# SwiGLU input products by seven block products instead of eight, on a kernel of two decoder layers

## The chip, the cores and the metric

The kernel runs on one core of a Trainium2 chip, as one program. The metric is device time in microseconds (us), the median of repeated runs. A core has five engines with a queue of instructions each, which run in order and wait for one another through semaphores: TensorE (PE in the profile; PEld is its weight load), VectorE (DVE), ScalarE (ACT), GpSimd (POOL) and SyncE (SP), which here issues the transfers (DMA).

## The reference, cut to what matters

Two layers, each of four stages with a LayerNorm behind each: SwiGLU, a mixer of three attention kinds, cross attention, SwiGLU. 512 tokens, 1024 model columns, 2816 hidden columns, all in float32.

```python
D_MODEL, SEQ, DEPTH = 1024, 512, 2
D_FF = ((8 * D_MODEL // 3 + 255) // 256) * 256          # 2816

def swiglu(x, w_in, w_out):
    a, b = jnp.split(x @ w_in, 2, axis=-1)
    return (jax.nn.silu(a) * b) @ w_out

for l in range(DEPTH):
    x = layer_norm(ALPHA * x + 0.5 * swiglu(x, ffn1_w_in[l], ffn1_w_out[l]), ln_g[l, 0], ln_b[l, 0])
    x = layer_norm(ALPHA * x + hybrid_mixer(x, ...), ln_g[l, 1], ln_b[l, 1])
    x = layer_norm(ALPHA * x + cross_attention(x, mem, ...), ln_g[l, 2], ln_b[l, 2])
    x = layer_norm(ALPHA * x + 0.5 * swiglu(x, ffn2_w_in[l], ffn2_w_out[l]), ln_g[l, 3], ln_b[l, 3])
```

## The kernel before, in words

*Products.* A float32 operand is split into two tiles of type fp32r: H, the rounded value (ScalarE's cast), and L, the rest (VectorE's subtraction). A product is then three matmuls, H with H, H with L and L with H (`mm3`). The weight of a matmul is a 128 x 128 block, its moving operand up to 512 columns wide.

*FFN stage (`Ffn`).* The activations stand transposed, `xTH` and `xTL`: 128 partitions x 8 row tiles x 512 tokens. The 5632 columns of `w_in` are taken in column tiles of 128, 22 of the gate part and 22 of the linear part. Per column tile `w_cols` fetches a raw tile (1 MB holds two column tiles; three buffers, `RAW`), `prep` makes `wH` and `wL` (four buffers each), and `proj_T` runs 8 x 3 matmuls of 512 columns into one PSUM bank (`ps`). `act` then applies silu to the gate bank, multiplies by the linear bank into a scratch tile `scr`, and splits the result into `hH` and `hL`.

*Output product (`out_proj`).* Hidden tiles are the weights now, `w_out` rows move, 512 columns at a time, in two column halves c. In the second half the last four groups are run token tile by token tile, so that the LayerNorm of token tiles 0 and 1 (`ln_half`, `ln_norm`) and their transposes (`transpose_x`) run under the remaining matmuls.

*Stage borders (`enter`).* The next stage's `early` runs its first four column tiles on tokens 0 to 255 while tokens 256 to 511 are still in LayerNorm; their transposes are put between. In `early` the subtraction that makes `wL` is shared, half on VectorE and half on GpSimd (`share`). At the very start `load_x` fetches x in halves, and `prefetch` the first weight tile in halves between them, with ScalarE's and VectorE's work on it pinned to its place in the order.

*What sets the order.* The framework's scheduler orders each engine's instructions by its own model of their times; a wait of one instruction holds all that stand behind it on that engine. Beside the first FFN runs a thread (`consts`, stepped in `tick`) that builds the mixer's bias table: eight heads, each a small matmul (`hot`, `rb`), a copy into the one buffer `F`, and two transfers (`biasD`, `biasT`).

Of the kernel before, what the change touches and what calls it, by code (L numbers as in the profile page):

```python
# [525 lines left out]
class Ffn:  # L526


    def __init__(self, net, l, w_in, w_out, lni):
# [2 lines left out]
        self.start = False

    def cols(self, f, part, share=False):
        if f < 2 and self.start:
            return self.net.w_cols((self.tag, part), self.w_in, part * DFF + f * P, n=P, share=share, pin=f == 0)
        return self.net.w_cols((self.tag, part), self.w_in, part * DFF + f * P, f % 2, share=share)

    def prefetch(self, h):

        n, nc = self.net, self.net.nc
        self.start = True
        if h == 0:
            self.raw0 = n.wp.tile([P, KT, P], F32, tag="raw", name=n.nm("raw"), bufs=RAW)
            self.W0 = [n.wp.tile([P, KT, P], F32R, tag=f"w{i}", name=n.nm(f"w{i}"), bufs=4) for i in "HL"]
        ks = slice(4 * h, 4 * h + 4)
        raw, (H, L) = self.raw0[:, ks], self.W0
        nc.sync.dma_start(raw, self.w_in[h * 512:(h + 1) * 512, 0:P].rearrange("(k p) n -> p k n", p=P))
# [3 lines left out]
    def early(self):  # L552
        n = self.net
        self.first = []
        for f in range(2):
# [720 lines left out]
```

## Time and profile before

| | |
|---|---|
| median of 3 runs | 2267.9 us (2267.69 to 2268.06) |
| the profiled execution, its own time | 2267.45 us |
| its span, first to last instruction | 2265.7 us |
| granted TensorE clock, mean | 0.998 |
| input products of one FFN, 782 to 1010 us | TensorE busy 228.00, VectorE 80.26, ScalarE 67.84 us |
| output product of that FFN, 1010 to 1130 us | TensorE busy 120.00, VectorE 39.17, ScalarE 22.11 us |

Busy times of an engine count its instructions from start to end; matmuls overlap in the pipeline, so TensorE's rate is read from the distance of starts. The four FFN stages lie at the start, at about 774 to 1138, 1138 to 1502 and 1896 to the end. Nearly all instructions of VectorE, ScalarE and GpSimd have one line, L121, a wrapper's, and all matmuls L194: groups are told apart by the tiles' names.

### The profile page before, as it was taken

The numbers are of one execution on the slowest core, as the hardware profiler recorded it, in microseconds if no ns is written. First come the engines' busy times: TensorE is split into PE (matmuls) and PEld (weight loads), VectorE is DVE, ScalarE is ACT, GpSimd is POOL, SyncE is SP. The second block draws the span as 40 slices with busy tenths as digits, with TensorE's granted clock in tenths as the row PEclk, the third lists the DMA queues.
The fourth block names the chain that finished last, engine by engine and source line by source line (L and its number), as shares of the span: only waits on it lengthen the run. The fifth ranks groups of instructions, "written<-read, shape, count | busy, mean of one in ns | idle before, by whom it ended". The sixth has DMA issues, their size and how long they took to land.

```text
span 2265.7 us, 27710 instructions
## 1 busy us (share of the span) xinstructions
PE 2243.9 (99%) x11360; PEld 1896.5 (84%) x11360; DVE 1082.0 (48%) x1696; ACT 756.5 (33%) x1217; POOL 178.9 (8%) x254
## 2 busy tenths in 40 slices
PE   9999999999999999999999999999999999999998
PEld 8788888888788888888888888888887888888887
DVE  3333335677565633332453333367776656333334
ACT  3222212457524232221132222124674333322211
POOL 1000001251010100000010000013300101000000
PEclk9999999999999999999999999999999999999999
DMA  7655333232432365653266553332233314656431
GB/s 252 220 189 195 130 102 103 68 93 82 124 99 69 112 223 187 199 167 107 84 206 200 188 195 112 102 95 80 88 113 94 112 57 155 199 188 201 150 103 47
DMA packets 273251, 310.97 MB, mean 137 GB/s; under 512 B 6330, under 2 KB 231898, under 8 KB 273124
## 3 DMA queue, kind: packets, MB, share of 16 engines
q1 hardware_dynamic: 273124, 309.20, 42.3%
q8 instruction: 89, 1.46, 0.3%
q14 instruction: 38, 0.31, 0.0%
HBM read 305.51 MB, written 3.67 MB: 136 GB/s over the span
## 4 chain that ended last, share of the span: by engine, by line
PE 90%; DVE 6%; issue 1%; POOL 1%; ACT 1%; DMA 0%; DVEq 0%; SPq 0%; ACTq 0%; POOLq 0%
PE ps L194 88%; PE ps L199 2%; DVE wL L121 1%; DVE x_nat L121 1%; DVE st L121 1%; DVE xTL L121 1%; POOL mlrs L121 1%; DVE Cb L121 0%; DMA x_nat<-in_x_dram 0%; ACT e L121 0%; DVE stL L121 0%; DVE mlst L121 0%; DVE hid L121 0%; ACT xTH L121 0%; DVE memT L121 0%
## 5 line engine op out<-in xcount | busy, mean ns | idle before, releaser
L121 DVE TENSOR_TENSOR wL<-raw,wH 128x1024 fp32r<-128x1024 f32 (+2 forms) x387 | 462.2, 1195 | 722.5 <-ACT wH L121 708.5
L121 ACT CAST wH<-raw 128x1024 fp32r<-128x1024 f32 (+2 forms) x387 | 403.3, 1046 | 1167.1 <-PE ps L194 833.0
L194 PE MATMUL ps<-xTH,wH 128*128 128x512 f32 (+1 forms) x2000 | 728.9, 365 | 1.0 <-ACT sc L121 1.0
L194 PE MATMUL ps<-xTL,wH 128*128 128x512 f32 (+1 forms) x2000 | 726.2, 363 | 2.7 <-DVE xTL L121 2.7
L194 PE MATMUL ps<-xTH,wL 128*128 128x512 f32 (+1 forms) x2000 | 725.4, 363 | 0.0
L194 PEld LDWEIGHTS ps<-xTL,wH 128*128 128x128 f32 x2000 | 378.3, 189 | 61.1 <-DVE xTL L121 5.2
L194 PEld LDWEIGHTS ps<-xTH,wH 128*128 128x128 f32 x2000 | 378.1, 189 | 59.2 <-ACT sc L121 1.2
L194 PEld LDWEIGHTS ps<-xTH,wL 128*128 128x128 f32 x2000 | 378.2, 189 | 58.7
L194 PE MATMUL ps<-wH,hH 128*128 128x512 f32 x704 | 274.8, 390 | 0.0
L194 PE MATMUL ps<-wH,hL 128*128 128x512 f32 x704 | 274.3, 390 | 0.0
L194 PE MATMUL ps<-wL,hH 128*128 128x512 f32 x704 | 274.2, 390 | 0.0
L121 DVE TENSOR_TENSOR scr<-scr,ps 128x512 f32<-128x512 f32 x88 | 60.5, 687 | 274.8 <-PE ps L194 272.7
L121 POOL TENSOR_TENSOR rs<-ve,mhalf 128x1 f32<-128x1 f32 x32 | 29.7, 927 | 1771.5 <-DVE ve L121 1771.5
L194 PEld LDWEIGHTS ps<-wH,hL 128*128 128x128 f32 x704 | 132.2, 188 | 27.5
L194 PEld LDWEIGHTS ps<-wL,hH 128*128 128x128 f32 x704 | 132.2, 188 | 27.3
L194 PEld LDWEIGHTS ps<-wH,hH 128*128 128x128 f32 x704 | 132.2, 188 | 27.0
L121 ACT CAST xTH<-ps 128x512 fp32r<-128x512 f32 x64 | 34.8, 589 | 153.5 <-PE ps L199 152.9
L194 PE MATMUL ps<-wH,oT 128*128 128x512 f32 x256 | 81.8, 392 | 0.0
L121 DVE SCALAR_TENSOR_TENSOR x_nat<-ps,x_nat 128x512 f32<-128x512 f32 x64 | 43.6, 686 | 44.9 <-PE ps L194 44.4
L121 DVE TENSOR_TENSOR hL<-scr,hH 128x512 fp32r<-128x512 f32 x88 | 60.2, 684 | 0.0
L194 PEld LDWEIGHTS ps<-wH,oT 128*128 128x128 f32 x256 | 48.1, 188 | 9.7
L121 ACT CAST hH<-scr 128x512 fp32r<-128x512 f32 x88 | 54.6, 620 | 0.0
(222 smaller groups left out, 2229.7 us busy)
## 6 DMA issues: line engine op xcount, KB each, us to landing
raw<-in_ffn_w_in_dram SPq DMA_DIRECT2D x172, 1024.0 KB, 5.1
raw<-in_ffn_w_out_dram SPq DMA_DIRECT2D x40, 1024.0 KB, 5.0
raw<-in_xattn_w_kv_dram SPq DMA_DIRECT2D x16, 1024.0 KB, 5.4
raw<-in_mix_w_in_dram SPq DMA_DIRECT2D x18, 512.0 KB, 5.7
raw<-in_mix_w_in_dram SPq DMA_DIRECT2D x8, 1024.0 KB, 5.2
raw<-in_mix_w_out_dram SPq DMA_DIRECT2D x16, 512.0 KB, 4.7
raw<-in_xattn_w_q_dram SPq DMA_DIRECT2D x8, 1024.0 KB, 5.1
raw<-in_xattn_w_o_dram SPq DMA_DIRECT2D x8, 1024.0 KB, 5.0
```

The costliest lines, as they stand in the source:

```text
L121: return f(*a, **k)
L194: self.nc.tensor.matmul(out, l, r, start=start, stop=stop, **k)
L199: self.nc.tensor.transpose(out, i, ident)
```

## The change

The input product of an FFN is cut in two along its columns (gate part a, linear part b), its rows (1: rows 0 to 511, 2: 512 to 1023) and its tokens (1: 0 to 255, 2: 256 to 511). Of 2 x 2 x 2 = 8 block products, Strassen's scheme (in Winograd's form) makes 7, with sums of blocks as operands. It is done for a group q of 256 gate and 256 linear columns, eleven groups (`Q`). The blocks of w are a1, a2, b1, b2; with s = b1 + b2 the products, each of 2 x 4 x 3 matmuls of 256 columns, are, in the order of the loop in `body`:

| name here | weight side | token side | goes to |
|---|---|---|---|
| X1 | a1 | B11 | gate, tokens 1 (kept as `p1`) |
| W | s = b1 + b2 | T1 | bank W |
| Y2 | s - a1 | T2 | bank Y, then + `p1`, copied to `u2` |
| R | b2 of the group before | T4 | its bank Y: linear, tokens 1 |
| X2 | a2 | B21 | gate, tokens 1, then silu (`gate1`) |
| L | a2 - (s - a1) of the group before | B22 | its bank W: with `u2` the gate, tokens 2 |
| Y3 | a1 - b1 | T3 | bank Y, copied to `u3`, + W: linear, tokens 2 |

So VectorE gets four additions or subtractions of 128 x 1024 per group (s; b1 = a1 - b1; s - a1; a2 - s) and sums of banks (`u2`, `u3`, Y + `p1`), and per FFN the token side's combinations T1 to T4, which `second` makes from token tiles 2 and 3 when they have been transposed. Groups 0 to 3 have X1 and X2 done in `early` (eight products of tokens 1 in place of four column tiles). The hidden values stay in float32, tile `h` per group, and are split into `hH` and `hL` in the output product's first column half. The weight tiles come in two transfers each; the pinning in `prefetch` is gone; `enter` is called when the stage's pools are closed; and the mixer's constant `chunk1` is filled in each mixer rather than once.

```diff
-        if nxt is not None:
-            self.enter(nxt)
     def enter(self, nxt):
+        if nxt is None:
+            return
         last = self.last
         for i, _ in enumerate(nxt.early()):
             self.hold = last
             if i < 2:
-                self.transpose_x(2 + i)
+                nxt.second(2 + i)
...
-        self.chunk1 = c.tile([MLH, S], F32, name="chunk1")
-        nc.gpsimd.memset(self.chunk1, 1.0)
-        nc.gpsimd.memset(self.chunk1.rearrange("h (c n) -> h c n", c=NT)[:, :, 0:1], 0.0)
...
+    EARLY = 4
+    HT = 256
+    Q = FT // 2
...
+    def open(self):
+        n = self.net
+        self.ctx, self.inner = ExitStack(), ExitStack()
+        self.fp = self.ctx.enter_context(n.tc.tile_pool(name=n.nm("ffn"), bufs=1))
+        self.h = {}
+        self.ip = self.inner.enter_context(n.tc.tile_pool(name=n.nm("ffnin"), bufs=1))
+        self.p1 = [self.ip.tile([P, S], F32, name=n.nm("p1")) for _ in range(self.EARLY)]
+        self.sw = self.ip.tile([P, 4, 256], F32, name=n.nm("sw"))
+        self.T = [[self.ip.tile([P, 4, self.HT], F32R, name=n.nm("T")) for _ in range(2)] for _ in range(3)]
...
+    def load(self, q, half):
+        r = self.raw()
+        for part in range(2):
+            self.net.nc.sync.dma_start(r[:, part], self.block(q, part, half))
+        return r[:, 0], r[:, 1]
...
+    def right(self, x):
+        xs = self.net.xTH, self.net.xTL
+        lo, hi, t1, t2 = slice(0, 4), slice(4, 8), slice(0, self.HT), slice(self.HT, S)
+        if x in ("T2", "T3", "T4"):
+            return self.T[int(x[1]) - 2]
+        k, t = {"B11": (lo, t1), "B21": (hi, t1), "B22": (hi, t2), "T1": (lo, t2)}[x]
+        return [m[:, k, t] for m in xs]
+    def product(self, bank, raw, x, start, share=False):
+        n = self.net
+        H, L = n.prep(raw, [4, 256], share)
+        xH, xL = self.right(x)
+        for j in range(2):
+            js = slice(j * P, (j + 1) * P)
+            o = bank[:, j * self.HT:(j + 1) * self.HT]
+            for k in range(4):
+                n.mm3(o, H[:, k, js], L[:, k, js], xH[:, k], xL[:, k], start and j + k == 0, k == 3, skip_group_check=True)
+            n.tick()
...
+    def two(self, name, dt=F32):
+        return self.fp.tile([P, 2, S], dt, tag="h", name=self.net.nm(name), bufs=self.Q + 1)
+    def hid(self, q, t):
+        if q not in self.h:
+            self.h[q] = self.two("h")
+        return self.h[q][:, :, t * self.HT:(t + 1) * self.HT]
...
-        n.tc.keep_in_program_order(nc.scalar.copy(H[:, ks], raw))
-        n.tc.keep_in_program_order(nc.vector.tensor_sub(L[:, ks], raw, H[:, ks].bitcast(F32)))
...
+        self.open()
+        for q in range(self.EARLY):
+            a = self.first if q == 0 else None
+            if a is None:
+                a = self.raw()
+                for h in range(2):
+                    nc.sync.dma_start(a[:, h], self.block(q, 0, h))
+            b = n.bank()
+            self.product(b, a[:, 0], "B11", True, True)
+            nc.scalar.copy(self.p1[q], b)
+            self.product(b, a[:, 1], "B21", False, True)
+            self.gate1(q, b)
+            yield
...
+    def second(self, t):
+        n, nc = self.net, self.net.nc
+        V = nc.vector
+        bs = [n.bank() for _ in range(2)]
+        for h in range(2):
+            for k in range(4):
+                kk = 4 * h + k
+                n.tp(bs[h][:, k * P:(k + 1) * P], n.x_nat[:, t, kk * P:(kk + 1) * P])
+        b1, b2 = [b.rearrange("p (k n) -> p k n", k=4) for b in bs]
+        ts, t1 = slice(t * P, (t + 1) * P), slice((t - 2) * P, (t - 1) * P)
+        tmp = [w[:, i].rearrange("p (k n) -> p k n", k=4) for w in (self.two("tmp"), self.two("tmp")) for i in range(2)]
+        r1, T2, T3, T4 = tmp
+        (H11, L11), (H21, L21) = self.right("B11"), self.right("B21")
+        n.split(n.xTH[:, 4:8, ts], n.xTL[:, 4:8, ts], b2)
+        nc.scalar.copy(r1, b1)
+        V.tensor_sub(T3, b2, r1)
+        V.tensor_sub(r1, r1, H11[:, :, t1].bitcast(F32))
+        V.tensor_sub(r1, r1, L11[:, :, t1].bitcast(F32))
+        n.split(n.xTH[:, 0:4, ts], n.xTL[:, 0:4, ts], r1)
+        V.tensor_sub(T2, b2, r1)
+        n.split(*[m[:, :, t1] for m in self.T[0]], T2)
+        V.tensor_sub(T4, H21[:, :, t1].bitcast(F32), T2)
+        V.tensor_add(T4, T4, L21[:, :, t1].bitcast(F32))
+        n.split(*[m[:, :, t1] for m in self.T[1]], T3)
+        n.split(*[m[:, :, t1] for m in self.T[2]], T4)
...
-        with n.tc.tile_pool(name=n.nm("ffn"), bufs=1) as fp:
-            hH = fp.tile([P, FT, S], F32R, name=n.nm("hH"))
-            hL = fp.tile([P, FT, S], F32R, name=n.nm("hL"))
-            def act(f, pa, pb):
-                s = n.scr()
-                nc.scalar.activation(s, pa, AF.Silu)
-                nc.vector.tensor_mul(s, s, pb)
-                n.split(hH[:, f], hL[:, f], s)
-            for f in range(FT):
-                bs = []
-                for part in range(2):
-                    if f < 2:
-                        W, b = self.first[2 * f + part]
-                        n.proj_T(b, W, 256, 512)
-                    else:
-                        W, b = self.cols(f, part), n.bank()
-                        n.proj_T(b, W, 0, S)
-                    bs.append(b)
-                act(f, *bs)
...
+        V, ACT = nc.vector, nc.scalar
+        prev = None
+        def rest(r):
+            q, Y, b2 = r["q"], r["Y"], r["b2"]
+            self.product(Y, b2, "T4", False)
+            V.tensor_mul(self.hid(q, 0), self.hid(q, 0), self.pair(Y))
+        def last(r):
+            q, W, u2, u3 = r["q"], r["W"], r["u2"], r["u3"]
+            self.product(W, r["s4"], "B22", False)
+            V.tensor_add(u2, W, u2)
+            ACT.activation(self.hid(q, 1), self.pair(u2), AF.Silu)
+            V.tensor_mul(self.hid(q, 1), self.hid(q, 1), self.pair(u3))
+        for q in range(self.Q):
+            a1, b1 = self.load(q, 0)
+            a2, b2 = self.load(q, 1)
+            s = self.sw
+            V.tensor_add(s, b1, b2)
+            p1 = self.p1[q % self.EARLY]
+            if q >= self.EARLY:
+                X = n.bank()
+                self.product(X, a1, "B11", True)
+                ACT.copy(p1, X)
+            W, Y = n.bank(), n.bank()
+            self.product(W, s, "T1", True)
+            V.tensor_sub(b1, a1, b1)
+            V.tensor_sub(s, s, a1)
+            self.product(Y, s, "T2", True)
+            V.tensor_add(Y, Y, p1)
+            u2 = n.scr()
+            ACT.copy(u2, Y)
+            if prev:
+                rest(prev)
+            if q >= self.EARLY:
+                self.product(X, a2, "B21", False)
+                self.gate1(q, X)
+            V.tensor_sub(a2, a2, s)
+            if prev:
+                last(prev)
+            self.product(Y, b1, "T3", False)
+            u3 = n.scr()
+            ACT.copy(u3, Y)
+            V.tensor_add(u3, W, u3)
+            prev = dict(q=q, Y=Y, W=W, b2=b2, s4=a2, u2=u2, u3=u3)
+        rest(prev)
+        last(prev)
+        self.inner.close()
+        with n.tc.tile_pool(name=n.nm("ffnh"), bufs=1) as hp:
+            hs = {}
+            def wsrc(k0, k, c):
+                if c == 0:
+                    q = k0 // 2
+                    hs[q] = hp.tile([P, 2, S], F32R, name=n.nm("hH")), self.two("hL", F32R)
+                    n.split(*hs[q], self.h[q])
+                return n.w_rows(self.tag, self.w_out, k0, k, c * 512, FT)
+            n.out_proj(FT, lambda f, t: [m[:, f % 2, t * P:(t + 1) * P] for m in hs[f // 2]], wsrc, 0.5 / ALPHA,
+                       self.l, self.lni, nxt)
+        self.ctx.close()
+        n.enter(nxt)
...
+        chunk1 = row("chunk1")
+        G.memset(chunk1, 1.0)
+        G.memset(chunks(chunk1)[:, :, 0:1], 0.0)
         nb = row("nb")
-        V.tensor_tensor_scan(nb, n.chunk1, e, 0.0, ALU.mult, ALU.add)
+        V.tensor_tensor_scan(nb, chunk1, e, 0.0, ALU.mult, ALU.add)
```

What the scheduler makes of it. VectorE in the middle of an FFN, before: `wL` for each column tile, and between them, for a gate and a linear tile together, `scr`, silu times the linear bank, and its split.

```order
L121 TENSOR_TENSOR wL_7010<-raw_7007,wH_7009 128x1024
L121 TENSOR_TENSOR scr_6935<-scr_6935,ps_6910 128x512
L121 TENSOR_TENSOR wL_7041<-raw_7038,wH_7040 128x1024
L121 TENSOR_TENSOR hL_6565<-scr_6935,hH_6564 128x512
L121 TENSOR_TENSOR wL_7077<-raw_7074,wH_7076 128x1024
```

Now, in the second FFN from the end of group 0 to group 2: `scr_7785` is u2 of group 0 (it waits for product L of group 0), `h_7462` that group's gate times u3, `sw_7392` is s, `raw_7981` b1 of group 2, `scr_7978` u3 of group 1, `wL_7991` is for product W of group 2, `wL_8021` for its Y2.

```order
L121 TENSOR_TENSOR scr_7785<-ps_7724,scr_7785 128x512
L121 TENSOR_TENSOR h_7462<-h_7462,scr_7816 128x2x256
L121 TENSOR_TENSOR sw_7392<-raw_7981,raw_7984 128x1024
L121 TENSOR_TENSOR raw_7981<-raw_7981 128x1024
L121 TENSOR_TENSOR scr_7978<-ps_7826,scr_7978 128x512
L121 TENSOR_TENSOR wL_7991<-sw_7392,wH_7990 128x1024
L121 TENSOR_TENSOR sw_7392<-sw_7392,raw_7981 128x1024
L121 TENSOR_TENSOR raw_7984<-raw_7984,sw_7392 128x1024
L121 TENSOR_TENSOR wL_8021<-sw_7392,wH_8020 128x1024
```

Three weight splits with two operations between them have become a run of nine in which the weight split that TensorE needs next stands sixth. On TensorE, L of group 0, Y3 of group 1 and W of group 2 follow each other.

ScalarE at the start of the kernel, before: the casts of the first weight tile (`wH_95`, in halves) stand around those of the transposed x.

```order
L121 CAST wH_95<-raw_94 128x512
L121 CAST xTH_91<-ps_100 128x4x128
L121 CAST xTH_91<-ps_107 128x4x128
L121 CAST wH_95<-raw_94 128x512
L121 CAST xTH_91<-ps_118 128x4x128
```

Now:

```order
L121 CAST wH_144<-raw_94 128x1024
L121 CAST wH_174<-raw_94 128x1024
L121 CAST wH_209<-raw_205 128x1024
L121 CAST xTH_91<-ps_96 128x4x128
L121 CAST xTH_91<-ps_103 128x4x128
```

Three weight casts, of which the third reads the second raw tile (group 1), have moved ahead of the first cast of x.

VectorE where the first FFN leaves `early`, now (before, the second token half's `xTL` stood there with nothing but weight halves around it): `raw_460` and `raw_463` are the raw tiles of group 0, `tmp` and `T` belong to `second`.

```order
L121 TENSOR_TENSOR wL_401<-raw_366,wH_400 128x512
L121 TENSOR_TENSOR sw_136<-raw_460,raw_463 128x1024
L121 TENSOR_TENSOR raw_460<-raw_460 128x1024
L121 TENSOR_TENSOR wL_470<-sw_136,wH_469 128x1024
L121 TENSOR_TENSOR sw_136<-sw_136,raw_460 128x1024
L121 TENSOR_TENSOR xTL_92<-ps_337,xTH_91 128x4x128
L121 TENSOR_TENSOR tmp_347<-ps_337,tmp_346 128x512
L121 TENSOR_TENSOR raw_463<-raw_463,sw_136 128x1024
```

The sums of group 0's weights, which wait for its transfers, stand ahead of the whole of `second` there.

More of the change, by code (lines that the diff above doesn't have):

```diff
@@ L435, in load_x @@
             if i >= 2:
-                self.transpose_x(i)
+                nxt.second(i)
             if i in (1, 2):
@@ L531, in __init__ @@
         self.tag = f"ffn{l}{lni}"
[L532 to L537, printed above, removed]
-    def prefetch(self, h):
-        n, nc = self.net, self.net.nc
[L542 to L548, printed above, removed]
-        n.tc.keep_in_program_order(nc.scalar.copy(H[:, ks], raw))
-        n.tc.keep_in_program_order(nc.vector.tensor_sub(L[:, ks], raw, H[:, ks].bitcast(F32)))
@@ L552, in early @@
[L552 to L555, printed above, removed]
-            for part in range(2):
-                W = getattr(self, "W0", None) if f + part == 0 else None
-                W, b = W or self.cols(f, part, True), n.bank()
-                n.proj_T(b, W, 0, 256)
-                self.first.append((W, b))
-                yield
+        self.first = None
+    def open(self):
[7 more added lines that the diff above has]
+        self.T = [[self.ip.tile([P, 4, self.HT], F32R, name=n.nm("T")) for _ in range(2)] for _ in range(3)]
@@ new lines, in block, with raw @@
+    def block(self, q, part, half):
+        c0 = part * DFF + 256 * q
+        return self.w_in[half * 512:half * 512 + 512, c0:c0 + 256].rearrange("(k p) n -> p k n", p=P)
+    def raw(self):
+        n = self.net
+        return n.wp.tile([P, 2, 4, 256], F32, tag="raw", name=n.nm("raw"), bufs=RAW)
+    def load(self, q, half):
[3 more added lines that the diff above has]
+        return r[:, 0], r[:, 1]
@@ new lines, in prefetch @@
+    def prefetch(self, h):
+        if h == 0:
+            self.first = self.raw()
+        self.net.nc.sync.dma_start(self.first[:, h], self.block(0, 0, h))
+    def right(self, x):
[5 more added lines that the diff above has]
+        return [m[:, k, t] for m in xs]
@@ new lines, in hid, with pair, gate1, early @@
+    def hid(self, q, t):
+        if q not in self.h:
+            self.h[q] = self.two("h")
+        return self.h[q][:, :, t * self.HT:(t + 1) * self.HT]
+    @staticmethod
+    def pair(b):
+        return b.rearrange("p (f n) -> p f n", f=2)
+    def gate1(self, q, bank):
+        self.net.nc.scalar.activation(self.hid(q, 0), self.pair(bank), AF.Silu)
+    def early(self):
+        n, nc = self.net, self.net.nc
+        self.open()
[11 more added lines that the diff above has]
+            yield
@@ L595, in __init__, with second @@
         self.w_in, self.w_out = net.A["mix_w_in"][l], net.A["mix_w_out"][l]
+    def second(self, t):
+        self.net.transpose_x(t)
     def early(self):
@@ L707, in body @@
             n.mx_ctx.close()
+        n.enter(nxt)
     def stack(self, b, scale, parts):
@@ L1145, in memory, with second @@
                 n.split(*n.mv[m][c], bs[m])
+    def second(self, t):
+        self.net.transpose_x(t)
     def early(self):
@@ L1186, in body @@
         del n.mk
+        n.enter(nxt)
     def head(self, h):
```

4 lines of the change are left out of this document (1 added, 3 removed).

## The prediction

> **What bounds the kernel now.** I read the page's busy times and chain of waits first, then the timeline inside one FFN's input products, then the groups with shapes kept apart, and last the start and one stage border.
>
> ```profile
> span 2265.7 us, 27710 instructions
> PE 2243.9 (99%) x11360; PEld 1896.5 (84%) x11360; DVE 1082.0 (48%) x1696; ACT 756.5 (33%) x1217; POOL 178.9 (8%) x254
> PE 90%; DVE 6%; issue 1%; POOL 1%; ACT 1%; DMA 0%; DVEq 0%; SPq 0%; ACTq 0%; POOLq 0%
> ```
>
> TensorE is 90% of the chain: work that leaves it shortens the kernel for as long as nobody makes it wait. Inside the input products (timeline; start and duration in us, in brackets the idle time before and who ended it):
>
> ```profile
> 798.82 0.28 PE L194 MATMUL ps<-xTL,wH 128*128 128x256 f32 x1
> 798.94 0.28 PE L194 MATMUL ps<-xTH,wL 128*128 128x256 f32 x1
> 799.06 0.40 PE L194 MATMUL ps<-xTH,wH 128*128 128x512 f32 x1
> 799.33 0.69 DVE L121 TENSOR_TENSOR scr<-scr,ps 128x512 f32<-128x512 f32 x1 [0.72 <-PE ps L194]
> 800.14 0.61 ACT L121 CAST hH<-scr 128x512 fp32r<-128x512 f32 x1
> 800.27 1.23 DVE L121 TENSOR_TENSOR wL<-raw,wH 128x1024 fp32r<-128x1024 f32 x1 [0.25 <-ACT wH L121]
> 801.41 0.68 DVE L121 TENSOR_TENSOR hL<-scr,hH 128x512 fp32r<-128x512 f32 x1
> ...
> 804.54 1.05 ACT L121 CAST wH<-raw 128x1024 fp32r<-128x1024 f32 x1 [3.79 <-PE ps L194]
> 805.50 0.59 ACT L121 ACTIVATE scr<-ps 128x512 f32<-128x512 f32 x1
> 805.63 1.23 DVE L121 TENSOR_TENSOR wL<-raw,wH 128x1024 fp32r<-128x1024 f32 x1 [3.54 <-ACT wH L121]
> 809.98 1.05 ACT L121 CAST wH<-raw 128x1024 fp32r<-128x1024 f32 x1 [3.90 <-issue]
> ```
>
> Prices from here. A 256-column matmul starts every 0.12 us. One column tile, 24 matmuls of 512 columns, takes 809.98 - 804.54 = 5.44 us, 0.2267 each: two halves cost 0.24, 6% more than one whole. A 1024-wide VectorE subtraction takes 1.23, the next independent one starts after 1.14 (800.27 to 801.41), so 0.09 overlaps: 0.60 for 512 independent elements, 0.72 where the next needs the result. The first reader of a finished bank starts 0.27 after the next product does (799.06 to 799.33). ScalarE to VectorE: 0.04. VectorE idles 3.5 us per tile: it hides everything today.
>
> ```profile
> L121 DVE TENSOR_TENSOR wL<-raw,wH 128x1024 fp32r<-128x1024 f32 x346 | 424.6, 1228 | 694.8 <-ACT wH L121 680.8 <-PE ps L199 1.7 <-PE ps L194 1.2
> L121 DVE TENSOR_TENSOR scr<-scr,ps 128x512 f32<-128x512 f32 x88 | 60.5, 687 | 274.8 <-PE ps L194 272.7 <-ACT scr L121 2.1
> L121 DVE TENSOR_TENSOR wL<-raw,wH 128x512 fp32r<-128x512 f32 x33 | 29.8, 904 | 10.1 <-ACT wH L121 10.1
> L121 DVE TENSOR_TENSOR lg<-lg,swden 128x512 f32<-128x512 f32 x24 | 15.0, 685 | 0.1
> L121 POOL TENSOR_TENSOR wL<-raw,wH 128x512 fp32r<-128x512 f32 x31 | 48.5, 1578 | 30.5 <-ACT wH L121 25.8 <-PE ps L194 4.7
> ```
>
> (Groups: count, total and mean ns, idle before.) A plain fp32 operation on two SBUF operands (lg) costs 685 ns, no less than the fp32r one.
>
> **What leaves.** Per FFN before: 40 tiles whole, 4 in halves: 40 x 5.44 + 192 x 0.12 = 240.6 us. After: 11 groups x 7 products x 24 x 0.12 = 221.8. Saved 18.9, four times 75.5 us: an eighth less multiplying, nearly half of it given back to the narrower matmul. The output stage's matmuls stay as they are; there the split of h moves from 22 pieces beside the input products to 11 pieces of 1024 beside the first half of the output product: 2 x 1.14 us of VectorE per 24 x 0.2267 = 5.4 us group, covered; without cover 11 x 1.2. Weight transfers halve (each tile was fetched twice, for TensorE's bound worth nothing).
>
> **What comes in.** VectorE's work per group rises to seven weight splits, four adds of 1024 and five operations of 512: 11 x 1.14 + 5 x 0.60 = 15.5 us at best, against 20.2 us of seven products and 14.4 of the five in groups 0 to 3 (there 9 x 1.14 + 3.0 = 13.3). It fits by sum. The order decides, because each engine runs its queue in order.
>
> *Groups 1 to 3.* Zero is the end of product L (B22). TensorE goes on with Y3 (2.88 us) and reaches W's third matmul, the first that needs wL, at 3.12. VectorE's queue, as the order quoted above has it: u2 0.27-0.96; h, after ScalarE's silu of 0.62, 1.66-2.35; s 2.26-3.49; b1, which overwrites what s reads, 3.52-4.75; u3 4.66-5.35; W's wL 5.26-6.49. TensorE waits 3.44 and ends W at 9.20. Then s-=a1 to 7.75, a2-=s to 9.01, Y2's wL to 10.15; its third matmul (R's first two go ahead) is due at 9.68: 0.54 more. Together 4.0 us, at two places in each FFN: 8 x 4.0 = 32.0. Behind these lines stand R, L and Y3, whose wL come in time.
>
> *Group 3 to 4 and on.* X1 (2.88) stands between Y3 and W: W's wL is due at 6.00, ready at 6.56, Y2's at 9.68 and 10.18: 1.06, four times 4.2. From group 5 on h comes after s, so its silu is not waited for, and a2-=s comes later in the queue: W's wL at 5.61, in time; s-=a1 to 6.88, cast to 7.97, Y2's wL 9.24 against 9.12. I take 0.4 us a group (0 to 1.5, the ends being no wait and one 1024 operation more), 6 x 4 x 0.4 = 9.6; the turn into the output stage 0.3 x 4 = 1.2.
>
> *Entering an FFN from another stage (three).* A border today:
>
> ```profile
> 1134.90 1.44 POOL L121 TENSOR_TENSOR wL<-raw,wH 128x512 fp32r<-128x512 f32 x1
> 1135.11 2.44 DVE L121 SCALAR_TENSOR_TENSOR x_nat<-x_nat,rs,scr 128x512 f32<-128x512 f32 x2
> ...
> 1138.16 0.28 PE L194 MATMUL ps<-xTH,wH 128*128 128x256 f32 x1
> ...
> 1143.80 1.41 DVE L121 SCALAR_TENSOR_TENSOR x_nat<-x_nat,rs,scr 128x512 f32<-128x512 f32 x2
> ```
>
> ```profile
> 777.34 0.87 PE ps L199 x8
> 778.22 2.87 PE ps L194 x24
> ```
>
> (The second fence is the chain: eight transposes 0.87, 24 matmuls 2.87.) LayerNorm ends 7.0 us after the first early product begins. Then VectorE has 26 operations of 512, 22 of them or so from `second`, and s, b1 and W's wL: 26 x 0.66 + 3.65 = 20.8, so W's wL at 27.8. TensorE, with 8 x 2.88 + 16 transposes 1.74, is there at 25.0. Eight GpSimd half splits run beside it; next to one, the pair at 1135.11 took 2.44 against 1.41 at 1143.80. Up to 3.2 us of that comes on top: wait 2.8 to 6.0, I take 4.0. Group 0 has no older group to fill in: Y2's wL 0.8 late, then Y3 waits for bank end, add and copy (0.27 + 0.69 + 0.59 + 0.1 = 1.65), W of group 1 for its transfer and wL 3.2, Y2 0.55: 6.2. Three times 10.2 = 30.6.
>
> *The start.*
>
> ```profile
> 4.69 1.10 PE L199 MATMUL ps<-ident,x_nat 128*128 128x128 f32 x8 [0.23 <-DMA x_nat<-in_x_dram]
> 7.68 1.58 PE L199 MATMUL ps<-ident,x_nat 128*128 128x128 f32 x8 [1.89 <-DMA x_nat<-in_x_dram]
> 9.27 0.41 PE L194 MATMUL ps<-xTL,wH 128*128 128x256 f32 x1
> 10.32 1.05 ACT L121 CAST wH<-raw 128x1024 fp32r<-128x1024 f32 x1 [0.17 <-DMA raw<-in_ffn_w_in_dram]
> 13.41 1.05 ACT L121 CAST wH<-raw 128x1024 fp32r<-128x1024 f32 x1 [2.05 <-DMA raw<-in_ffn_w_in_dram]
> ```
>
> Transfers land in issue order: 512 KB at 4.69, 2048 at 10.3, 3072 at 13.4. In the new order three weight casts precede the transposed x on ScalarE, the third waiting for the transfer that completes 2560 KB, at 11.9; cast, VectorE's half split, two xTL: 14.9 against 9.27, 5.6 lost. Then s of group 0 stands on VectorE ahead of all of `second` and waits for a transfer that cannot be issued before the third early tile is split (26.4 by the same steps; landing 31.5 by the 5.1 below). From there 7 operations of 1024 and 17 of 512 to W's xTL: 19.6, so 51.1; TensorE is there at 41.5: 9.6. Group 1's s waits in the same way, 2.5. Together 17.7.
>
> ```profile
> raw<-in_ffn_w_in_dram SPq DMA_DIRECT2D x172, 1024.0 KB, 5.1
> ```
>
> ```profile
> 44.72 0.57 SPq L481 DMA_DIRECT2D biasD<-F  x1
> 50.34 0.34 SPq L482 DMA_DIRECT2D biasT<-biasD  x1
> 51.23 0.56 SPq L481 DMA_DIRECT2D biasD<-F  x1
> 56.95 0.32 SPq L482 DMA_DIRECT2D biasT<-biasD  x1
> ```
>
> In this first FFN eight copies of the bias table F run through one buffer, 6.5 us apart (44.72 to 51.23). They stand on VectorE's queue now between the adds, three of them closer than that: each then holds the adds up by some 3 us, 8 in all (0 if their gaps fall into VectorE's idle time, 14 if none does). The GpSimd fill of chunk1, now in each mixer, is 0.6 us beside other work; bounds 0 and 1.2 for both, taken 0.
>
> **Sum** against the profiled execution (2267.45, 1.75 over its span, 0.45 under the runs' median): -75.5 + 32.0 + 4.2 + 9.6 + 1.2 + 30.6 + 17.7 + 8.0 = +27.8, so 2295 us, slower. The waits, 103, outweigh the matmuls that leave.
>
> **Rivals.** *The clock drops at the waits (slower still).*
>
> ```profile
> 7.60:8.90 1.30, 1.22 (x8) 1.23 (x9) 1.28 (x3) 0.34 (x1) 0.00 (x0) 0.71 1.16 343
> 8.90:10.00 1.10, 1.10 (x7) 1.10 (x6) 0.87 (x3) 1.10 (x3) 0.00 (x0) 0.50 1.10 361
> 10.00:11.40 1.40, 1.40 (x9) 1.40 (x8) 1.11 (x3) 1.20 (x2) 0.00 (x0) 0.50 1.08 335
> ```
>
> (Busy time by stretch; the third column from the end is the granted clock.) After an idle stretch of 1.89 us among transposes the clock was 0.71, then 0.50 until 11.4: 0.38 + 0.55 + 0.70 = 1.6 us lost. Four waits per FFN are longer than that 1.89: 16 x 1.6 = 26, giving 2321. Against it: here the waits stand among dense matmuls. [...]
>
> *The second halves land late.* From group 4 on the transfer of a2 and b2 is issued when Y3's wL is done, 4.8 us before L ends, and s wants it 0.87 after: 5.7 us for a 5.1 us landing. If sharing the queue with a1 and b1 costs 1.6 more, each group waits 1 us, 24 in all: 2319.
>
> *VectorE's new adds are quicker (faster).* If the 1024 adds and the 512 ones between plain fp32 tiles took half, the wait in groups 1 to 3 would be 2.0 instead of 4.0, at the borders 4.3 instead of 10.2, from group 4 on 0.2 instead of 0.4, at the start 12 and with F 4: 16 + 13 + 5 + 1 + 1 + 12 + 4 = 52 against 75.5, 2244. It turns at about 0.85 us for a 1024 add. The lg row, 685 ns, speaks against it. [...]
>
> **How the numbers follow.** 0.2% is 4.5 us, about what can be told from no change here. Forecast as summed 0.52 (2270 to 2310), clock 0.18, late halves 0.11, quick adds 0.10, and 0.09 for waits that just eat the gain (2258 to 2272; half faster, a third same). Slower 0.81 + 0.02, same 0.03, faster 0.14. The range 2255 to 2325 leaves out the quick adds and the worst of clock and late halves together, about 2 in 10; the forecast's own is 2270 to 2310.
>
> **What would show it.** TensorE's busy time near 2170 with over 100 us of idle ended by VectorE's wL in the four input stages; waits of some 3.4 us before W in groups 1 to 3; xTH casts after 12 us at the start; 256-column matmuls 0.12 apart; clock 1.00 but for the start. Input stages without such gaps would make it wrong, and so would a granted clock of 0.5 after them.

## The result: 2334.2 us, 2.9% slower

| | before | after |
|---|---|---|
| median of the runs | 2267.98 us (2267.69 to 2268.09) | 2334.18 us (2331.32 to 2336.04) |
| ratio to before | | 1.0291 (95% interval 1.0273 to 1.0309) |
| forecast | | 2295 us (2255 to 2325) |
| granted TensorE clock, mean | 0.998 | 0.982 |

The sign was right; of the 66 us lost the forecast had 28. The page of the changed kernel, the rows that answer to those shown of before:

```profile
span 2334.3 us, 34202 instructions
PE 2221.7 (95%) x14144; PEld 2004.8 (86%) x14144; DVE 1559.5 (67%) x2163; ACT 975.8 (42%) x1468; POOL 207.7 (9%) x273
PEclk8999999999999999999998999999999999899999
```

TensorE is busy for 22 us less than before although 75 us of matmuls left; in part this is because some of them now run at a lower clock (the slices with an 8; 0.50 in the windows of 3.41 us below). Its idle time is 2334.3 - 2221.7 = 112.6 us against 21.8. The forecast had named over 100 us of idle, which came, and a busy time near 2170, which did not. Who ended it (waits of TensorE: total, times, longest):

```profile
PE ps L194 <- ACT wH L121: 27.4, 27, 5.4
PE ps L194 <- DVE wL L121: 23.5, 25, 1.9
PE ps L194 <- DVE xTL L121: 12.9, 9, 3.1
PE ps L194 <- ACT scr L121: 10.5, 7, 1.6
PE ps L194 <- ACT xTH L121: 10.4, 3, 6.1
PE ps L194 <- ACT p L121: 8.1, 7, 1.5
```

The second FFN from the same LayerNorm of one stage to that of the next (windows; length, then busy time of TensorE, its weight loads, VectorE, ScalarE, GpSimd, and the granted clock, third from the end), first before, then after:

```profile
778.22:1142.70 364.48, 364.12 (x1714) 305.78 (x1714) 135.13 (x159) 97.56 (x120) 9.67 (x8) 1.00 0.50 162
```

```profile
799.92:1181.33 381.41, 358.72 (x2413) 332.53 (x2412) 254.74 (x276) 152.13 (x182) 16.13 (x12) 0.98 0.33 105
```

16.9 us longer, where the forecast had 3.1 (-18.9 + 10.2 + 8.0 + 1.06 + 6 x 0.4 + 0.3). The first FFN is not where the forecast missed: measured in the same way it takes 19.4 us more, and the forecast had 18.6. Inside the second, groups 2 and 3 of the input products. VectorE's and TensorE's timeline of the changed kernel:

```profile
858.79 1.23 DVE L121 TENSOR_TENSOR sw<-raw,raw 128x1024 f32<-128x1024 f32 x1 [1.26 <-DMA raw<-in_ffn_w_in_dram]
...
877.21 0.69 DVE L121 TENSOR_TENSOR scr<-ps,scr 128x512 f32<-128x512 f32 x1 [2.19 <-PE ps L194]
878.60 0.69 DVE L121 TENSOR_TENSOR h<-h,scr 128x512 f32<-128x512 f32 x1 [0.70 <-ACT h L121]
879.21 1.22 DVE L121 TENSOR_TENSOR sw<-raw,raw 128x1024 f32<-128x1024 f32 x1
880.46 1.22 DVE L121 TENSOR_TENSOR raw<-raw 128x1024 f32<-128x1024 f32 x1
881.61 0.68 DVE L121 TENSOR_TENSOR scr<-ps,scr 128x512 f32<-128x512 f32 x1
882.21 1.22 DVE L121 TENSOR_TENSOR wL<-sw,wH 128x1024 fp32r<-128x1024 f32 x1
```

```profile
861.21 0.39 PE L194 MATMUL ps<-xTH,wH 128*128 128x256 f32 x1 [2.92 <-ACT wH L121]
863.07 0.58 PE L194 MATMUL ps<-xTH,wL 128*128 128x256 f32 x1 [1.36 <-DVE wL L121]
881.67 0.39 PE L194 MATMUL ps<-xTH,wH 128*128 128x256 f32 x1 [1.62 <-ACT wH L121]
883.48 0.58 PE L194 MATMUL ps<-xTH,wL 128*128 128x256 f32 x1 [1.30 <-DVE wL L121]
```

The rows from 877.21 on are the forecast's chain, operation for operation: u2, h, s, b1, u3, W's wL, with wL starting 5.27 us behind the end of L (u2 starts 0.27 behind it; the forecast had 5.26) and TensorE idle for 1.62 + 1.30 us. But s follows s after 20.4 us where the forecast's group takes 14.4 + 4.0 = 18.4. Two things are new: s of group 2 waits 1.26 us for a transfer, and the clock falls to 0.50 at both W, from 862.10 to 868.93 us (windows of 3.41 us below) and from 882.58 to 889.41:

```profile
858.69:862.10 3.41, 0.50 (x2) 0.30 (x2) 3.27 (x4) 1.27 (x2) 0.00 (x0) 1.00 0.00 0
862.10:865.51 3.41, 2.44 (x11) 2.44 (x12) 3.34 (x4) 1.15 (x2) 0.00 (x0) 0.50 0.00 0
865.51:868.93 3.42, 3.42 (x18) 3.42 (x17) 3.42 (x4) 2.71 (x3) 0.00 (x0) 0.50 0.00 0
```

In the whole trace such stretches of half clock, 3.41 or 6.83 us each, take away 42 us (1 minus the granted clock, summed over windows of 1 us) against 4 before. It looked as if the forecast's waits were right and the clock, its first rival, came on top. The experiments say that this is half of it.

### The profile page after: what moved, and what is told of

Its sections match the earlier page's. It is cut to its first block, busy times and chain, and to the rows that moved or that the text cites. A ratio compares the mean times of both kernels' runs of the same rounds, so it can differ in the third digit from the quotient of the medians.

```text
span 2334.3 us, 34202 instructions
## 1 busy us (share of the span) xinstructions
PE 2221.7 (95%) x14144; PEld 2004.8 (86%) x14144; DVE 1559.5 (67%) x2163; ACT 975.8 (42%) x1468; POOL 207.7 (9%) x273
## 5 line engine op out<-in xcount | busy, mean ns | idle before, releaser
L121 ACT CAST wH<-raw 128x1024 fp32r<-128x1024 f32 (+1 forms) x430 | 442.2, 1048 | 651.4 <-PE ps L194 503.9
L194 PE MATMUL ps<-xTH,wH 128*128 128x256 f32 (+1 forms) x1872 | 569.3, 304 | 44.1 <-ACT wH L121 24.2
L194 PE MATMUL ps<-xTH,wL 128*128 128x256 f32 (+1 forms) x1872 | 565.7, 303 | 20.4 <-DVE wL L121 20.4
L194 PE MATMUL ps<-xTL,wH 128*128 128x256 f32 (+1 forms) x1872 | 563.9, 301 | 12.9 <-DVE xTL L121 12.9
L194 PE MATMUL ps<-T,wH 128*128 128x256 f32 x2112 | 393.8, 287 | 14.0 <-ACT scr L121 10.5
L194 PEld LDWEIGHTS ps<-T,wH 128*128 128x128 f32 x2112 | 331.6, 194 | 20.9 <-ACT scr L121 11.9
L194 PE MATMUL ps<-T,wL 128*128 128x256 f32 x1056 | 295.6, 286 | 3.1 <-DVE wL L121 3.1
L194 PEld LDWEIGHTS ps<-T,wL 128*128 128x128 f32 x1056 | 200.4, 192 | 4.1 <-DVE wL L121 3.7
L121 ACT CAST wH<-sw 128x1024 fp32r<-128x1024 f32 x88 | 92.6, 1052 | 99.0 <-DVE sw L121 98.8
L121 DVE TENSOR_TENSOR wL<-sw,wH 128x1024 fp32r<-128x1024 f32 x88 | 107.3, 1220 | 33.1 <-ACT wH L121 33.1
```

What stands on the lines that cost most here:

```text
L121: return f(*a, **k)
L194: self.nc.tensor.matmul(out, l, r, start=start, stop=stop, **k)
```

## The experiments

Times are medians, each with its ratio to the kernel before and the 95% interval; "less" is against the changed kernel's 2334.2. The kernel before ran beside each set and gave 2267.5 to 2268.7, so that a difference of 1 us between sets means nothing.

**Fill the waits (`warm`).** `fill` puts matmuls of no use ahead of a product, into its own bank; they keep TensorE busy and shorten nobody's wait.

```diff
+            if 0 < q < self.EARLY:
+                n.fill(W, 22)
             self.product(W, s, "T1", True)
...
+            if q == 0 and n.lastmm is not None:
+                n.fill(b, 20)
             self.product(b, a[:, 0], "B11", True, True)
```

> Twenty-two extra 256-column matmuls (2.64 us) into W's own bank ahead of W in groups 1 to 3 of each FFN, and 20 (2.4 us) ahead of the first early product of the three FFNs that follow another stage; their results are overwritten. No wait of VectorE or ScalarE is shortened. Theory A (the forecast's waits are right and what was left out is the clock, which falls to a half for 3.41 or 6.83 us behind any stretch of 3.41 us in which TensorE idles for more than about 1.6): in the last three FFNs nine half-clock stretches, 54.6 us in all of the changed kernel's trace, go, half of the time TensorE is busy in them: 2334 - 25 = 2309 (2302 to 2316), mean granted clock 0.993 or more. Theory B (the waits themselves or the products are longer than priced, and the low clock stands where nobody needs it): 2334 within 4.

Measured 2330.2 us (1.0270, 1.0254 to 1.0285). The mean clock rose to 0.993 and the loss by it fell from 42 to 16 us, but the time only by 4, as theory B has it. (The fillers cost something too: with them the LayerNorm behind the first FFN comes 1.5 us later.) VectorE's timeline of the second FFN shows who took the rest:

```profile
866.76 3.49 DVE L121 TENSOR_TENSOR wL<-raw,wH 128x1024 fp32r<-128x1024 f32 x3
...
878.75 1.23 DVE L121 TENSOR_TENSOR sw<-raw,raw 128x1024 f32<-128x1024 f32 x1 [1.32 <-DMA raw<-in_ffn_w_in_dram]
```

The third of the three splits at 866.76 ends at 870.25 and frees the raw buffer into which the next second halves go; s of the next group has them 8.5 us later. Then it is 11.3 us from s to the end of the third split. 8.5 + 11.3 = 19.8 us, and TensorE's products are in neither part. The transfers of 838 to 884 us in the changed kernel, in 40 slices of 1.15 us (busy tenths, then GB/s):

```profile
DMA  1000000000199999300000000000899997000000
GB/s 39 0 0 0 0 0 0 0 0 0 28 267 330 386 348 355 110 13 0 0 0 0 0 0 0 0 0 13 224 338 345 301 373 241 2 0 0 0 0 0
```

Two bursts of 2 MB, both tiles of a group in one, with nothing between: the queue has no free buffer. Theory C, formed here: with three raw buffers this loop paces groups 1 to 3, however long TensorE works. It takes 19.8 us here and 18.9 in the last FFN, so that it stands just under the changed kernel's 20.4; there s of groups 3 and 4 waits for no transfer.

**Move X1 (`x1late`).** X2 alone is made early for groups 1 to 6, X1 of these groups in the loop, so that 17.3 us of products and not 14.4 lie in a group's time.

```diff
-    EARLY = 4
+    EARLY = 1
+    LATE = 6
...
+                self.product(b, a[:, 1], "B21", True, True)
+                nc.scalar.copy(self.hid(q, 0), self.pair(b))
...
-            if q >= self.EARLY:
+            if q > self.LATE:
                 self.product(X, a2, "B21", False)
                 self.gate1(q, X)
+            elif q:
+                V.tensor_add(self.hid(q, 0), self.hid(q, 0), self.pair(X))
+                ACT.activation(self.hid(q, 0), self.hid(q, 0), AF.Silu)
```

> The eight early products are X1 and X2 of group 0 and X2 alone of groups 1 to 6 (kept in the tile h, the gate sum X1 + X2 made there by one more VectorE addition of 512); X1 of groups 1 to 6 stands in the loop between Y3 and W. Same products, same token side. Theory A (the waits of groups 1 to 3 come from VectorE's chain from L to W's wL having 2.88 us of TensorE's work beside it instead of 5.76): waits of groups 1 to 3, 10.3 us in the second FFN, fall to 0.3 to 1.0 a group, and the half-clock stretches there go: 2334 - 33 - 22 = 2279 (2270 to 2290). Theory B (VectorE's work, 0.6 us a group more here, or the transfer of a2 and b2 sets the pace in any order): 2315 to 2334.

Measured 2327.2 us (1.0260, 1.0245 to 1.0276); theory A fell. In the second FFN s follows s after 19.3 to 20.3 us from group 2 to group 6, as it did with one product less, and VectorE waits for transfers there more often (from 820 to 960 us, first the changed kernel, then this one: total, times, longest):

```profile
DVE sw L121 <- DMA raw<-in_ffn_w_in_dram: 4.1, 2, 2.8
```

```profile
DVE sw L121 <- DMA raw<-in_ffn_w_in_dram: 6.3, 7, 1.4
```

**Put the casts of x first at the start (`start`).**

```diff
             for t in range(2):
                 self.transpose_half(t, h)
+            self.holds.append(self.last)
+        self.hold = self.holds.pop(0)
...
             nc.scalar.copy(self.p1[q], b)
+            if getattr(n, "holds", None):
+                n.hold = n.holds.pop(0)
```

> At the start alone, ScalarE's casts of the transposed x are put ahead of the early weight casts again. Theory A (the start costs what was forecast, 5.6 us of late start and the half-clock stretch behind it): the first early product starts at 9.3 to 10 instead of 12.8, 5 to 9 us go, 2327 (2324 to 2330). Theory B (VectorE's and the transfers' work sets the first W at 51.3 us whenever the first product starts): the gap before W grows by what the start gains, 2334 within 2.

Measured 2329.3 us (1.0266, 1.0249 to 1.0283), 4.9 less. The first product starts at 11.6 us instead of 12.8, not at 9.3: its weight cast now stands behind all four casts of x. W of group 0 starts at 51.05 instead of 51.34 us, behind a gap of 8.37 instead of 6.11 us. So the gap took most of the gain back, as theory B has it. LayerNorm at the end of this FFN comes 3.1 us earlier (381.2 against 384.3) all the same, and the time lies in theory A's range; which later step gives these is not shown.

**Pauses of known length (`ladder`), in the kernel before.** `pause` is the chain of copies and the one matmul that waits for it.

```diff
+                        if part and f >= 4 and f % 2 == 0 and self.l + self.lni > 0:
+                            n.pause(bs[0], b, f // 2 - 2)
                         n.proj_T(b, W, 0, S)
```

> The kernel before, with a pause put into the dense matmuls of the last three FFNs at column tiles 4, 6, ..., 20: one extra matmul waits for a chain of ScalarE copies, zero to eight in the middle, that starts when the gate tile's bank is finished; about 1.7 to 3.7 us each, 27 pauses. Theory A (clock decided at the ends of fixed stretches of 3.41 us, halved for the next one where TensorE idled more than about 1.6 in it): pauses cut by such an end into two short pieces leave the clock alone, the others cost one stretch of 3.41 us at a half each, whatever their length; the edges of all stretches lie a multiple of 3.413 us apart. Theory B (only an idle stretch of 3.4 us or more halves the clock): only the longest one or two of each FFN do. Time by A 2268 + 73 of pauses + 15 x 1.7 = 2366, by B 2345.

Measured 2394.2 us (1.0553, 1.0532 to 1.0574), above both. The 27 pauses sum to 83.2 us, not 73; 19 were followed by half a clock, for 3.41 us, twice for 6.83. 83 + 21 x 1.7 = 119 of the 126 us lost; 7 stay open. The windows lie on the same grid of 3.41 us, a stretch and the one behind it:

```profile
1233.08:1236.49 3.41, 1.72 (x8) 1.47 (x9) 1.23 (x1) 1.64 (x4) 0.00 (x0) 1.00 0.37 111
1236.49:1239.91 3.42, 3.42 (x17) 2.83 (x16) 0.00 (x0) 0.00 (x0) 0.00 (x0) 1.00 0.89 295
2031.80:2035.21 3.41, 1.61 (x8) 1.07 (x7) 1.23 (x1) 1.90 (x4) 0.00 (x0) 1.00 0.57 195
2035.21:2038.62 3.41, 3.41 (x10) 2.63 (x9) 0.00 (x0) 0.00 (x0) 0.00 (x0) 0.50 0.83 266
```

Here 1.69 us of idle in a stretch left the clock alone, and 1.80 halved it in the next. A pause of 3.08 us that the grid cut into 1.60 and 1.47 cost no clock; one of 1.80 inside one stretch cost 1.7 us of it. Theory A of this run stands, though its time did not, and theory B's 3.4 us do not (1.80 was enough): in these pauses it was the share of a fixed stretch that counted.

**A fourth raw buffer (`raw4x`), in the last three FFNs.**

```diff
-        r = self.raw()
+        if q % 2 and half and self.l + self.lni:
+            r = self.ip.tile([P, 2, 4, 256], F32, tag="rawx", name=self.net.nm("raw"), bufs=1)
+        else:
+            r = self.raw()
```

> One raw buffer more (four instead of three) for the input products of the last three FFNs; the transfer of a group's second halves no longer waits until the product Y3 of the group before has been split. Theory C (formed after the run with fillers, in which s followed s every 19.8 us in groups 1 to 3 although TensorE had 14.4 us of products: the loop of buffer freed, 2 MB of transfers in 8.6 us, s, and 11.2 us of VectorE to the third split sets the pace there): groups 1 to 3 take 14.4 to 16.5 us instead of 19.8 to 20.4, the half-clock stretches there go, 3 x 3 x 4.5 = 40 less, 2294 (2286 to 2304). Theory D (VectorE's chain from the end of L to W's wL sets it, as forecast, 18.4 us a group): 3 x 3 x 1.8 = 16 less, 2318. Theory A (the clock): 2330.

Measured 2283.1 us (1.0067, 1.0051 to 1.0084): 51 us less, more than theory C gave. s of groups 2 and 3 in the second FFN:

```profile
848.73 1.23 DVE L121 TENSOR_TENSOR sw<-raw,raw 128x1024 f32<-128x1024 f32 x1 [0.26 <-DMA raw<-in_ffn_w_in_dram]
865.71 1.22 DVE L121 TENSOR_TENSOR sw<-raw,raw 128x1024 f32<-128x1024 f32 x1 [1.83 <-DMA raw<-in_ffn_w_in_dram]
```

17.0 us apart, and s still waits for its transfer. With the buffer, the framework's scheduler also put s ahead of u2 and h in VectorE's queue, so two things had changed.

**The fourth buffer with VectorE's old order (`raw4late`).** `follow` fixes the order of two instructions on an engine and nothing else; `done` is the last sum of `last`.

```diff
-            V.tensor_add(s, b1, b2)
+            i = V.tensor_add(s, b1, b2)
+            if q <= self.EARLY:
+                n.follow(i, done)
...
-                last(prev)
+                done = last(prev)
```

> The fourth raw buffer in the last three FFNs as in raw4x, with VectorE's order of the changed kernel kept in groups 0 to 4: s of a group behind the last sum of the group before the last. It tells the transfer itself from the place of s in VectorE's queue, which the fourth buffer had moved ahead by three to four operations. If the transfer alone set the pace: 2283 within 4. If the place of s in the queue does (the chain that the forecast priced, 4.0 us a wait): groups 1 to 3 at 18.4 us, 3 x 3 x 1.6 = 14 more than raw4x and the half-clock stretches of 3.4 us behind such waits, up to 3 x 3 x 1.7 = 15: 2297 to 2312.

Measured 2308.2 us (1.0174, 1.0157 to 1.0191), in the range for the place of s: 26 less than the changed kernel and 25 more than `raw4x`. The 26 are not the transfers alone. `done` is empty in group 1 and nothing is fixed from group 5 on, and there s moved ahead: in group 5 of the second FFN it starts at 909.89, before u2 at 913.43, where in the changed kernel it comes behind u2. Only groups 2 to 4 tell the transfers from the order, and little of the gain lies there. VectorE's sum behind product R, which waits for TensorE, in groups 0, 1 and 2 of the second FFN, first the changed kernel, then this one:

```profile
852.57 0.69 DVE L121 TENSOR_TENSOR h<-h,ps 128x512 f32<-128x512 f32 x1 [1.61 <-PE ps L194]
874.33 0.69 DVE L121 TENSOR_TENSOR h<-h,ps 128x512 f32<-128x512 f32 x1 [1.94 <-PE ps L194]
894.75 0.69 DVE L121 TENSOR_TENSOR h<-h,ps 128x512 f32<-128x512 f32 x1 [1.94 <-PE ps L194]
```

```profile
848.08 0.69 DVE L121 TENSOR_TENSOR h<-h,ps 128x512 f32<-128x512 f32 x1 [2.18 <-PE ps L194]
867.42 0.69 DVE L121 TENSOR_TENSOR h<-h,ps 128x512 f32<-128x512 f32 x1 [1.94 <-PE ps L194]
887.84 0.69 DVE L121 TENSOR_TENSOR h<-h,ps 128x512 f32<-128x512 f32 x1 [0.46 <-PE ps L194]
```

42.2 us for two groups against 39.8. Over the last three FFNs, between the profiled executions, 6.9 of 27.3 us gained lie between these rows, 11.6 ahead of them (W of group 1 above all, which in the second FFN waits 0.52 us instead of 1.62 + 1.23) and 8.8 behind.

And the last step, the waits of this kernel filled in groups 2 and 3 (`r4latewarm`):

```diff
+            if 1 < q < self.EARLY and self.l + self.lni:
+                n.fill(W, 16)
             self.product(W, s, "T1", True)
```

> raw4late (fourth buffer, VectorE's order of the changed kernel) with 16 extra matmuls (1.92 us) into W's own bank ahead of W in groups 2 and 3 of the last three FFNs; the waits there, 1.62 + 1.30 us, stay as long as they are. If the clock costs what it seems to once the transfers no longer set the pace: the half-clock stretches of 3.41 and 6.83 us go, 3 x 4.5 = 13 less than raw4late's 2308, 2295 (2291 to 2300), and groups 2 and 3 follow each other in the 17.6 to 18.4 us that the forecast's chain gives. If it costs nothing, as with three buffers (4 us in the run with fillers): 2304 to 2309.

Measured 2301.8 us (1.0153, 1.0136 to 1.0170): 6.4 less than `raw4late`, half of what was expected, and outside both ranges. But the distances are clean. s of groups 2, 3 and 4:

```profile
853.07 1.22 DVE L121 TENSOR_TENSOR sw<-raw,raw 128x1024 f32<-128x1024 f32 x1
871.45 1.22 DVE L121 TENSOR_TENSOR sw<-raw,raw 128x1024 f32<-128x1024 f32 x1
889.83 1.22 DVE L121 TENSOR_TENSOR sw<-raw,raw 128x1024 f32<-128x1024 f32 x1
```

18.38 and 18.38 us: 14.4 + 4.0, the forecast's own figure, once neither the transfers nor the clock stand in the way. From the sum behind R of group 0 to that of group 2, two groups, in us:

| | 2nd FFN | 3rd | 4th | sum |
|---|---|---|---|---|
| forecast, 2 x 18.4 | 36.8 | 36.8 | 36.8 | 110.4 |
| changed kernel | 42.18 | 40.86 | 42.17 | 125.2 |
| fillers alone (`warm`) | 39.65 | 39.71 | 37.76 | 117.1 |
| fourth buffer alone (`raw4late`) | 39.76 | 40.82 | 37.71 | 118.3 |
| both (`r4latewarm`) | 36.76 | 36.75 | 36.74 | 110.3 |
| fourth buffer, s ahead (`raw4x`) | 32.44 | 33.01 | 32.93 | 98.4 |

Of the 14.8 us by which the changed kernel overruns the forecast here, the fillers take 8.1 and the buffer 6.9: each about half, and only both together give the forecast's figure in all three FFNs. How much of the buffer's share is the clock again (the loss by it fell from 42 to 31 us with the buffer) is not separated.

**The entry (`entry`).** The changed kernel's waits for xTL, 12.9 us with a longest of 3.1 at each of the three borders into an FFN, were these before:

```profile
PE ps L194 <- DVE xTL L121: 2.7, 8, 0.4
```

VectorE of the changed kernel at the second FFN's entry:

```profile
790.11 3.50 DVE L121 SCALAR_TENSOR_TENSOR x_nat<-x_nat,rs,scr 128x512 f32<-128x512 f32 x2
793.53 2.35 DVE L121 TENSOR_TENSOR wL<-raw,wH 128x512 fp32r<-128x512 f32 x2
795.80 1.28 DVE L121 TENSOR_TENSOR xTL<-ps,xTH 128x512 fp32r<-128x512 f32 x2
```

Two half splits of the first weight tile stand ahead of xTL and GpSimd's two beside the LayerNorm, whose pair took 2.44 next to one. The edit puts the second one behind:

```diff
             nc.scalar.copy(self.p1[q], b)
+            if q == 0 and self.l + self.lni:
+                n.hold = n.last
```

> At the three borders into an FFN, the cast and split of group 0's second weight tile stand behind the splits of token tiles 0 and 1, so that one half split and not two runs on GpSimd beside VectorE's last LayerNorm operations. Theory E (the 3.09 us wait for xTL at each entry, 0.36 before, and the half-clock stretch of 3.41 us behind it belong to the missing 38 us): 3 x (2.7 + 1.7) = 13 less, 2321 (2317 to 2326). Rival: VectorE's work on token tiles 2 and 3 sets when W of group 0 can start, so that what the entry gains is waited for there: 2331 to 2335.

Measured 2321.9 us (1.0242, 1.0227 to 1.0257), 12.3 less; theory E's 13. The pair takes 2.44 again and TensorE waits 0.36 us:

```profile
792.03 0.39 PE L194 MATMUL ps<-xTL,wH 128*128 128x256 f32 x1 [0.36 <-DVE xTL L121]
```

**The copies p1 (`px`) and F (`aF`).** Two smaller suspects, each with one edit: X1 of the next group between X1 and X2, and `nc.scalar.copy(F[:, P:2 * P], b[:, :P])` in place of VectorE's copy.

> In the early products X1 of the next group stands between X1 and X2 of a group, so that nobody waits for the copy p1 of X1's bank (8.1 us in all, longest 1.5, in the changed kernel). Same products. Theory: 4 x 2.3 = 9 less, 2325. Rival: VectorE's work on token tiles 2 and 3 sets when W of group 0 can start, the gain is waited for there: 2331 to 2335.

> The eight copies of the bias table F in the first FFN are made by ScalarE instead of VectorE, nothing else. The forecast put 8 us on their standing in VectorE's queue (0 to 14): 2326 (2322 to 2330). Rival: they only shift into ScalarE's queue, or their waits lie in time in which VectorE waits for transfers anyway: 2334 within 3.

Measured 2330.9 us (1.0279, 1.0264 to 1.0294) and 2332.1 us (1.0284, 1.0269 to 1.0300): 3.3 and 2.1 less, with runs that overlap the changed kernel's. That the copies p1 are mostly covered by the wait for group 0's W, as the rival has it, fits but is not shown; with F's copies moved the LayerNorm of the last token tile behind the first FFN comes no earlier (406.5 against 406.3 us), so that nothing shows of the 8 us put on F.

**Together.** `x1r4` joins the late X1 and the fourth buffer in all four FFNs, `x1r4s` adds the start, `best` the entry.

> X2 alone made early for groups 1 to 6 and X1 in the loop, as in the run before, and the fourth raw buffer in all four FFNs. Theory C: the loop of transfers is gone, so that groups 1 to 6 follow TensorE's 17.3 us (17.3 to 18.3 a group instead of 19.3 to 20.3) and the later ones 20.2 to 20.5: 4 x 6 x 1.9 = 46 less than the 2327 of that run, 2281 (2272 to 2292). Theory D (VectorE's chain): within 10 of 2327.

> The run x1r4 with ScalarE's casts of the transposed x put ahead of the early weight casts at the start. Theory: the 4.9 us that this saved alone come off again where no transfer loop takes them back: 5 to 8 less than x1r4. Rival: the first FFN's second token tiles (transfers of x and VectorE's token sums) set the first W in any case: within 2 of x1r4.

> x1r4s (X2 alone early for groups 1 to 6, fourth raw buffer in all FFNs, the casts of x first at the start) with the order of the run entry at the three borders. Theory E: 3 x 4.4 = 13 less than x1r4s's 2254, 2241. Rival: what the entry gains is waited for at W of group 0, 2250 to 2254. Below the kernel before in either case.

Measured 2257.7 us (0.9956, 0.9941 to 0.9971), 2253.9 us (0.9938, 0.9924 to 0.9953) and 2248.6 us (0.9918, 0.9903 to 0.9933). In `x1r4` s follows s after 17.4 to 18.1 us from group 2 to group 7 of the second FFN, as theory C gave for 17.3 us of products; the total was 23 us below its forecast, which nothing here explains. It is 25 below `raw4x`, but 13.8 of these lie in the first FFN, where `raw4x` has no fourth buffer. The casts of x gave 3.8 and the entry 5.3, not 13: both fell between their theories. The page of `best`:

```profile
span 2248.4 us, 34265 instructions
PE 2186.8 (97%) x14144; PEld 1982.0 (88%) x14144; DVE 1574.4 (70%) x2187; ACT 981.8 (44%) x1492; POOL 207.0 (9%) x273
```

So the scheme does pay, 0.8%, when the transfers and the orders are made for it.

## Why the prediction was wrong

- **The matmuls, -75.5: right.** 256-column matmuls start 0.12 apart, and ScalarE's copies of p1, one for each later group, stand 20.44 us apart against the 20.16 + 0.4 of the forecast:

```profile
924.65 0.59 ACT L121 COPY p<-ps 128x512 f32<-128x512 f32 x1 [2.23 <-PE ps L194]
945.09 0.59 ACT L121 COPY p<-ps 128x512 f32<-128x512 f32 x1 [2.25 <-PE ps L194]
```

  With the fourth buffer these groups take 20.16 us (VectorE's sums behind R, `raw4late`), the products alone. So the 0.4 had the right size, but it goes with the buffer; the forecast had put it on VectorE's queue.
- **Groups 1 to 3, 8 x 4.0 = 32.0: the step that failed.** VectorE's chain was right to 0.02 us a group, and putting s ahead of it gave 25 us in three FFNs where the forecast had 24 (by some luck: part of the 25 is the clock, whose loss fell from 31 to 18 us). But the chain was taken as the only limit. The transfers were priced at a 5.1 us landing, for W of group 1 and from group 4 on; in groups 2 and 3 the forecast didn't ask when a raw buffer comes free. There both tiles of a group are fetched in one burst, 8.5 us from the freeing to s, and the loop of 19.8 us that this closes is longer than the forecast's 18.4. And the clock was taken as 1.00: it falls at the waits (to 0.50, for 6.83 us at each W of groups 2 and 3 of the last three FFNs), and the same chain takes 20.4. Together they cost 14.8 us in the last three FFNs.
- **The rival "the second halves land late": right in kind,** wrong in place and size. It was priced at 1 us a group from group 4 on, 24 in all; the buffer took about 9 us there in three FFNs, about 7 in groups 2 and 3, and about 12 ahead, at W of group 1, where the forecast had a wait for the transfer.
- **The rival "the clock drops at the waits": it happened,** with a granted clock of 0.5, which the forecast had named as a sign that it was wrong. Of the 42 us lost to it in the trace little came back: filling the waits gave 4 us beside three buffers and 6.4 beside four. In groups 2 and 3 it was worth 8.
- **The borders, 30.6: too low by the entry.** The forecast saw that GpSimd's half split slows VectorE's LayerNorm pair to 2.44 us, but not that two of them would now stand ahead of xTL: 12.3 us. W of group 0 was too high, 4.0 against 0.41 + 1.24 in the second FFN.
- **The turn into the output stage, 1.2: too low.** The last R waits 1.56 us in each FFN for a copy out of its bank, 6.2 in all, a wait that the forecast had priced at group 0 alone.
- **The start, 17.7, and F, 8.0: not right one by one.** Of the start 4.9 could be taken away, and nothing shows of F. That the first FFN takes 19.4 us more where the forecast had 18.6 is luck: its groups 2 and 3 take 20.7 and 23.8 us, not 18.4.
- **"VectorE's adds are quicker": wrong.** s takes 1.22 to 1.23 us, as priced.

Of the 38 us that the forecast lacks, 14.8 and 12.3 have a cause that a run shows, and 4 more, of the last three FFNs, stand in the rows of the last R. The remaining 7 or so, with W of group 0 priced too high on the other side, stay open. That these parts add up is not shown: the entry gave 12.3 us in one kernel and 5.3 in another.

## What to carry to other kernels

For a stage in which work per buffer shrinks, write down the loop buffer freed, transfer, first use, last use, and compare it with the compute of that same stretch; a loop that another stretch covers can be the limit here. Where two limits stand close together (20.4 and 19.8 us a group), taking one away alone shows little of either: take each away, then both. Look where a run gains before naming what it tested: one more buffer gave 26 us, of which 7 lay in the groups that it was meant for, and 51 where the scheduler was free to move the first user of the transfer ahead.
